# Opening stage of a two-layer hybrid trunk: remainders on VectorE, squares summed on TensorE, rotary angles first, loads in another order

## The chip, the cores and the metric

The kernel runs on one core of one Trainium2 chip. The metric is the device time of one execution in microseconds (us); lower is better. One core has TensorE (PE; its weight loads are listed apart as PEld), VectorE (DVE), ScalarE (ACT), GpSimd (POOL) and SyncE (SP), which here only issues the loads and stores.

## What is computed

Two layers; each is a mixer (latent attention and a state-space part side by side) and a SwiGLU, both behind an RMSNorm that is shifted and scaled by a modulation vector. Only the start of layer 0 bears on the change:

```python
ang = positions.astype(f32)[..., None] * inv_freq          # rotary angles
cos, sin = jnp.cos(ang), jnp.sin(ang)
c_act = jax.nn.silu(c)                                     # (1, 1024)
for l in range(2):
    mod = c_act @ w_ada[l] + b_ada[l]                      # w_ada: 1024 x 6144
    sh1, sc1, g1, sh2, sc2, g2 = jnp.split(mod, 6, axis=-1)
    h = rmsnorm(x, norm1_w[l]) * (1.0 + sc1) + sh1         # x: 512 x 1024
    x = x + g1 * hybrid_mixer(h, cos, sin, w_in[l], ...)   # begins with h @ w_in, 1024 x 1960
    h = rmsnorm(x, norm2_w[l]) * (1.0 + sc2) + sh2
    x = x + g2 * swiglu(h, w_gate_up[l], w_down[l])
```

## The kernel before

Activations lie transposed, xT[channel in a block of 128, block k = 0..7, row 0..511]. Every large product is taken in three matmuls: an f32 operand is split into a rounded part ("hi", hh, hik) and the remainder (lo, hl, lok), and hi·hi, hi·lo and lo·hi are added up in PSUM. ScalarE makes the rounded parts; the remainders are subtractions on VectorE or GpSimd.

The opening stage of layer 0 first loads c (cb, on all partitions) and x in two halves of 256 rows, squares x on ScalarE (sq), adds the squares on VectorE, sums over channels by a matmul with ones (st for the first half, nst for the second) and turns the sums into row scales (na, then rs). Matmuls of ones with ones (`warm`) fill TensorE in between. It then takes eight steps, k = 0..7, one for each block of channels:

- load two 512 KB tiles of w_ada (raws, blocks 8 + k and k) and a 404 KB slab of w_in (rawk);
- each raws is multiplied by cb and summed on VectorE into one column of mods; the bias is added, and gn = (1 + scale) · norm weight;
- ht = xT · gn · rs on VectorE; hh and hu, the rounded and the full hidden, on ScalarE; hl = hu − hh on GpSimd (step 0 does each of these per half of the rows);
- hik, the rounded slab, on ScalarE, and lok = rawk − hik on GpSimd;
- 21 matmuls into seven PSUM banks st: four chunks of 128 rows against the first 424 columns of the slab, and three column tiles of 128 against all 512 rows.

In step 2, `small_tables` makes the rotary angles (24 short operations on pf, ang, kk, kh, kl on VectorE, then three sines on ScalarE) and the mask mkb. After step 7 the mixer goes on with the tiles lo_7 and lo_8 (remainders of the next two weight tiles, on GpSimd), copies rw out of the banks, convolutions (xbc) and further products wps. SyncE issues all loads in the order of the program; a load waits there until its buffer is free (six buffers for raws, three for rawk and the later raw, three each for hi and lo).

Outside the parts that are pinned to program order, a scheduler orders the instructions of each engine when the kernel is built. At run time each engine takes its own in that order and waits by semaphores.

Of the kernel before, what the change touches and what calls it, by code (L numbers as in the profile page):

```python
# [71 lines left out]
    'KHV': 0,  # L72
# [3 lines left out]
P = 128  # L76
S = 512
# [68 lines left out]
class Kept:  # L146
    """an engine; while kept, its instructions stay in the order they are written in"""
# [19 lines left out]
class Stream:  # L167
    """steps for the tensor engine; a step yields the time from which on the next should find its data"""
# [9 lines left out]
def drive(te, streams, back):  # L178
    """the steps of all streams: next comes the first stream in the list whose step should find its data,
    and a step of back where there is none"""  # L180
    te.pinned = True
    while streams:
        for s in streams + [back]:
            if s.ready is not None and s.ready() <= te.now:
                s.step()
                break
        else:
            te.now = min(s.ready() for s in streams + [back] if s.ready is not None)
            assert te.now < INF
        streams = [s for s in streams if s.ready is not None]  # L190
    te.pinned = False
# [3 lines left out]
def trunk(ctx, tc, xin, cin, pos, eye, consts, small, wada, ws, out):  # L195
# [39 lines left out]
    tc.keep_in_program_order(nc.scalar.preload_act_table_set("silu_and_others"))  # L235
    nc.sync.dma_start(cb, cin.partition_broadcast(P))
    xload(HALVES[0])
    xload(HALVES[1])
    nc.sync.dma_start(sm[0], small[0])
# [12 lines left out]
    def small_tables():  # L252
        ve.tensor_copy(idb, ident)
        mk = kc[:, K_MASK:K_MASK + P]
        for i in range(4):
            tc.keep_in_program_order(ge.tensor_copy(mkb[:, i, :], mk))
# [3 lines left out]
        ang, kk, kh, kl = (tiny(nm, n, 1) for nm in ("ang", "kk", "kh", "kl"))  # L260
# [19 lines left out]
        ve.tensor_scalar(ang, ang, pi, -pi, op0=ALU.min, op1=ALU.max)  # L280
        v4 = lambda t: t.rearrange("p (c f) -> p c f", f=16)
# [3 lines left out]
        ve.tensor_copy(cs2[:, :, 1, :], cs2[:, :, 0, :])  # L285

# [82 lines left out]
    def rsqrt(y, x, scale, name, a=None, out=None):  # L369
        """y = (x * scale + EPS) ** -0.5: exp(-ln / 2) and a Newton step"""  # L370
        if a is None:
            a = tiny(f"na_{name}", x.free_size())
        se.activation(y, x, AF.Ln, scale=scale, bias=eps)
        se.activation(y, y, AF.Exp, scale=-0.5)
        if isinstance(scale, float):
            ve.scalar_tensor_tensor(a, x, EPS / scale, y, op0=ALU.add, op1=ALU.mult)
            ve.scalar_tensor_tensor(a, a, -0.5 * scale, y, op0=ALU.mult, op1=ALU.mult)
        else:
            ve.tensor_scalar(a, x, scale, EPS, op0=ALU.mult, op1=ALU.add)
            ve.scalar_tensor_tensor(a, a, -0.5, y, op0=ALU.mult, op1=ALU.mult)  # L380
            ve.tensor_tensor(a, a, y, op=ALU.mult)
        ve.scalar_tensor_tensor(y if out is None else out, a, 1.5, y, op0=ALU.add, op1=ALU.mult)

    class Norm:
        """adaLN over the columns of xT: squares added up tile by tile, then the row scale and the hidden"""
# [16 lines left out]
        def scale(self, sl, ps=None, rb=None):  # L402
            """(mean square + eps) ** -0.5 of the rows in sl, on all partitions"""
# [55 lines left out]
    def mixer(l, h, rows, first):  # L459
        s_ = sm[l]  # L460
        with tc.tile_pool(name=f"mx{l}", bufs=1) as mp:
# [14 lines left out]
            def decays():  # L476
                """time steps and decays, [step in chunk, (chunk, head)]"""
# [40 lines left out]
            def dense():  # L518
                """the rest of W_in, then the first half of the rows of W_out, tile by tile"""
# [56 lines left out]
            with tc.tile_pool(name=f"up{l}", bufs=2) as up, psum(f"u{l}", mm=2, ms=2, at=4):  # L576
# [3 lines left out]
                # latents, a chunk's rows on the partitions (their row scale follows after the up-projections)  # L580
# [33 lines left out]
                # rotary factors with the norm weights in them  # L614
# [7 lines left out]
                def rope(x, cw, sw, shape, name, re=ve):  # L622
                    """in place on x[..., 32]"""
# [109 lines left out]
            with tc.tile_pool(name=f"s2{l}", bufs=2) as sp, psum(f"v{l}", ms=2, sc=2, pt=1, op=1, mm=2):  # L733
# [12 lines left out]
                # attention over (chunk, heads), in three steps  # L746
# [34 lines left out]
                def values(c, h0, g):  # L781
                    """two heads at a time, one in each half of the columns of the array: channels on the partitions"""
# [39 lines left out]
                def norms():  # L822
                    """one over the sums of the probabilities, turned to where the channels are; then the products' split"""
# [19 lines left out]
                # the state space part, chunk by chunk  # L843
# [148 lines left out]
    def out_proj(l, mix, nrm, sl, kept):  # L992
        """one half of the rows; the weight tiles that lie on chip at its end are kept for the other half"""
# [93 lines left out]
    for l in range(L):  # L1087
        if l == 0:
            with tc.tile_pool(name="s0", bufs=6) as s0, psum("s", ms=1, st=NCH + NC0):
# [23 lines left out]

                def load(k):
# [178 lines left out]
```

## Time and profile before

| quantity | value |
|---|---|
| three timed runs | 1287.88 us median (1286.55 to 1293.02) |
| profiled execution | span 1284.9 us (the page gives its span alone) |
| PE busy | 1211.4 us, 94% of the span |
| DVE, ACT, POOL busy | 49%, 40%, 41% |
| chain that ended last | PE 38%, DVE 4%, ACT 2%, POOL 1%, DMA 1% |
| DMA | 162.34 MB, mean 126 GB/s |

The span is the time from the first to the last instruction of one profiled execution; the timed runs take some us more, since they hold what lies around it. Busy shares are means over all stages. The opening stage, up to the last matmul of step 7, takes the first 77.6 us.

### The profile page before, as it was taken

How to read it: one execution, taken by the hardware profiler on the slowest of the kernel's cores; microseconds unless marked ns; L12 is line 12 of the kernel's file. 1: busy time of each engine (PE TensorE's matmuls, PEld its weight loads, DVE VectorE, ACT ScalarE, POOL GpSimd, SP SyncE). 2: the span in 40 equal slices, each digit the busy share in tenths (PEclk: the TensorE clock that was granted, in tenths of full speed). 3: DMA queues.
4: the chain of work that ended last, by engine and by line, in shares of the span. 5: the costliest groups of instructions: out<-in, count | busy, mean ns of one | idle time of the engine just before them, and what ended most of it. 6: DMA issues, size and time to landing. Idle time of an engine off the chain costs nothing. (4 is left out here: it accounts for less than half of the span.)

```text
span 1284.9 us, 16463 instructions
## 1 busy us (share of the span) xinstructions
PE 1211.4 (94%) x6343; PEld 1005.1 (78%) x6344; DVE 634.1 (49%) x1128; ACT 519.9 (40%) x896; POOL 531.1 (41%) x310
## 2 busy tenths in 40 slices
PE   6889796889999999999998999979999999999998
PEld 6768674689888888888887887659988888888888
DVE  6979778879245545211128885576821111110100
ACT  4366774435322222222226668654532222222110
POOL 2651145263676666523333232346333333333231
PEclk9899898899999999999999899999999999999999
DMA  9433352464477777423223222103333332323331
GB/s 321 154 125 102 114 164 99 150 200 143 129 241 238 239 240 237 134 87 97 96 71 107 83 79 70 34 33 91 124 115 99 90 106 84 102 94 107 115 101 40
DMA packets 47855, 162.34 MB, mean 126 GB/s; under 512 B 5344, under 2 KB 8224, under 8 KB 47776
## 3 DMA queue, kind: packets, MB, share of 16 engines
q1 hardware_dynamic: 47776, 161.29, 38.8%
q8 instruction: 50, 0.82, 0.3%
q14 instruction: 29, 0.24, 0.1%
HBM read 159.14 MB, written 2.13 MB: 126 GB/s over the span
## 5 line engine op out<-in xcount | busy, mean ns | idle before, releaser
L292 POOL TENSOR_TENSOR lo<-raw,hi 128x1024 fp32r<-128x1024 f32 x108 | 272.6, 2524 | 338.6 <-ACT hi L156 338.5
L156 ACT CAST hi<-raw 128x1024 fp32r<-128x1024 f32 x179 | 188.0, 1051 | 500.8 <-issue 183.5
L140 PE MATMUL gup<-hl,hi 128*128 128x512 f32 (+1 forms) x736 | 280.4, 381 | 0.0
L140 PE MATMUL gup<-hh,lo 128*128 128x512 f32 (+1 forms) x736 | 279.9, 381 | 0.0
L140 PE MATMUL gup<-hh,hi 128*128 128x512 f32 (+1 forms) x736 | 278.6, 381 | 0.0
L156 DVE TENSOR_TENSOR lo<-raw,hi 128x1024 fp32r<-128x1024 f32 x71 | 88.9, 1253 | 152.6 <-ACT hi L156 150.8
L140 PEld LDWEIGHTS gup<-hh,lo 128*128 128x128 f32 x736 | 139.1, 189 | 26.5
L140 PEld LDWEIGHTS gup<-hl,hi 128*128 128x128 f32 x736 | 139.0, 189 | 26.0 <-DVE hl L156 0.2
L140 PEld LDWEIGHTS gup<-hh,hi 128*128 128x128 f32 x736 | 138.4, 189 | 26.2
L156 DVE SCALAR_TENSOR_TENSOR rawa<-rawa,cb 128x1024 f32<-128x1024 f32 x77 | 111.0, 1443 | 76.7 <-DMA rawa<-wada 76.5
L140 PE MATMUL dps<-ah,hi 128*128 128x512 f32 x308 | 121.8, 396 | 0.0
L140 PE MATMUL dps<-al,hi 128*128 128x512 f32 x308 | 121.8, 396 | 0.0
L140 PE MATMUL dps<-ah,lo 128*128 128x512 f32 x308 | 121.8, 396 | 0.0
L156 DVE TENSOR_TENSOR sg<-sg,gup 128x512 f32<-128x512 f32 x44 | 30.3, 688 | 179.6 <-PE gup L140 173.5
L440 POOL TENSOR_TENSOR al<-sg,ah 128x512 fp32r<-128x512 f32 x44 | 67.6, 1535 | 97.2 <-ACT ah L156 93.6
L140 PE MATMUL ops<-hh,hi 128*128 128x256 f32 x256 | 74.4, 290 | 3.1 <-ACT hi L156 1.5
L140 PE MATMUL ops<-hl,hi 128*128 128x256 f32 x256 | 72.5, 283 | 1.0 <-POOL hl L440 1.0
L140 PE MATMUL wps<-hh,hi 128*128 128x512 f32 x168 | 70.8, 422 | 2.4 <-DVE xbc L156 2.4
L140 PE MATMUL ops<-hh,lo 128*128 128x256 f32 x256 | 72.5, 283 | 0.3 <-POOL lo L292 0.3
L140 PEld LDWEIGHTS dps<-al,hi 128*128 128x128 f32 x308 | 57.9, 188 | 14.1
L140 PEld LDWEIGHTS dps<-ah,hi 128*128 128x128 f32 x308 | 57.9, 188 | 14.0
L140 PEld LDWEIGHTS dps<-ah,lo 128*128 128x128 f32 x308 | 57.9, 188 | 13.9
(303 smaller groups left out, 2103.3 us busy)
## 6 DMA issues: line engine op xcount, KB each, us to landing
raw<-ws SPq DMA_DIRECT2D x181, 512.0 KB, 3.5
rawa<-wada SPq DMA_DIRECT2D x80, 512.0 KB, 4.4
raws<-wada SPq DMA_DIRECT2D x16, 512.0 KB, 5.3
ar<-ard SPq DMA_DIRECT2D x8, 512.0 KB, 3.9
rawk<-ws SPq DMA_DIRECT2D x8, 404.0 KB, 5.4
xT<-xin SPq DMA_DIRECT2D x8, 256.0 KB, 5.9
out<-xT SPq DMA_DIRECT2D x7, 256.0 KB, 2.6
rawr<-ws SPq DMA_DIRECT2D x4, 424.0 KB, 3.2
```

Of the source, the lines that this page charges most:

```text
L140: self._put(self.tc.nc.tensor.matmul(out, lhsT, rhs, **kw), 4 * n if rhs.dtype == F32 else n)
L156: i = f(*args, **kw)
L292: (eng or ve).tensor_tensor(lo[:, :n], raw[:, :n], hi[:, :n].bitcast(F32), op=ALU.subtract)
L440: (eng or ve).tensor_tensor(lo, src, hi.bitcast(F32), op=ALU.subtract)
```

## The change

Only the opening stage's code is edited. The remainders hl and lok are made on VectorE; hl is taken from ht, its shift and hh in one instruction, so that hu is not made. The squares are no longer added on VectorE: TensorE sums eight blocks for each half, and VectorE makes half of the second half's squares. The angles are computed at the start, the sines before the table for logarithm and exponential is loaded, and gn takes one instruction with a prepared gb. Positions and frequencies are loaded first, then the first half of x, cb, the small weights and the second half of x. The third `warm` is gone.

```diff
+    nc.sync.dma_start(posi, pos)
+    nc.sync.dma_start(kc[:, K_FREQ:NK], consts[:, K_FREQ:NK])
+    xload(HALVES[0])
     nc.sync.dma_start(cb, cin.partition_broadcast(P))
-    xload(HALVES[0])
+    nc.sync.dma_start(sm[0], small[0])
     xload(HALVES[1])
-    nc.sync.dma_start(sm[0], small[0])
...
-                def stat(sl):
+                def squares(sl):
                     sq = s0.tile([P, KT, S // 2], F32, name=f"sq01{sl.start}", tag="sq", bufs=2)
                     for k in range(0, KT, 2):
-                        se.activation(sq[:, k:k + 2], xT[:, k:k + 2, sl], AF.Square)
-                        if k > 0:
-                            ve.tensor_tensor(sq[:, 0:2], sq[:, 0:2], sq[:, k:k + 2], op=ALU.add)
-                    for j in range(2):
-                        te.matmul((nst if sl.start else sps[-2])[:, 0:S // 2], ones, sq[:, j], start=j == 0, stop=j == 1)
+                        x = xT[:, k:k + 2, sl]
+                        if sl.start and k > 2:
+                            ve.tensor_tensor(sq[:, k:k + 2], x, x, op=ALU.mult)
+                        else:
+                            se.activation(sq[:, k:k + 2], x, AF.Square)
+                    return sq
+
+                def stat(sl, sq):
+                    for k in range(KT):
+                        te.matmul((nst if sl.start else sps[-2])[:, 0:S // 2], ones, sq[:, k], start=k == 0, stop=k == KT - 1)
...
                         ada1(0, t, s0.tile([P, 8, P], F32, name=f"raws{t}", tag="raws"))
-                        ada_fin(0, t, t + 1)
-                    return slab(wraw(f"k{k}"), wk0[k], f"k{k}", NS0, ge)
+                        m = mods[0][:, t:t + 1]
+                        if t < 8:
+                            ve.tensor_tensor(m, m, sm[0][:, C_BADA + t:C_BADA + t + 1], op=ALU.add)
+                        else:
+                            ve.scalar_tensor_tensor(gn[0][:, k:k + 1], m, nw1[:, k:k + 1], gb[:, k:k + 1], op0=ALU.mult, op1=ALU.add)
+                    return slab(wraw(f"k{k}"), wk0[k], f"k{k}", NS0)
...
+                angles()
                 warm(PLAN['WU'])
+                sq = squares(HALVES[0])
                 se.activation(cb, cb, AF.Silu)
-                stat(HALVES[0])
+                stat(HALVES[0], sq)
+                sq = squares(HALVES[1])
+                sines()
                 exp_ln_tables()
+                ve.scalar_tensor_tensor(gb, sm[0][:, C_BADA + 8:C_BADA + 16], 1.0, nw1, op0=ALU.add, op1=ALU.mult)
+                stat(HALVES[1], sq)
+                scale(HALVES[0])
+                scale(HALVES[1])
                 warm(PLAN['WV'])
-                scale(HALVES[0])
-                stat(HALVES[1])
-                scale(HALVES[1])
-                warm(PLAN['WW'])
...
                     for sl in HALVES if k == 0 else (FULL,):
-                        last = hid(0, 1, h, k, rs0[:, sl], sl, ge)
-                    for sl in HALVES if k < PLAN['KHV'] else (FULL,):
+                        last = hid(0, 1, h, k, rs0[:, sl], sl)
                         mms(k, w, sl)
                     if k == PLAN['STK']:
                         with tc.issue_after(last.ins):
-                            small_tables()
-                        exp_ln_tables()
+                            ve.tensor_copy(idb, ident)
+                            se.copy(cs2[:, :, 1, :], cs2[:, :, 0, :])
```

How the instructions stand then, at three places. VectorE, one step of the loop (raws13 and raws5 are the two w_ada tiles of step 5, ht015 its scaled x); before:

```order
L156 SCALAR_TENSOR_TENSOR raws13_459,mods0_92<-raws13_459,cb_69 128x1024
L156 TENSOR_TENSOR mods0_92<-mods0_92,sm0_72 128x1
L156 SCALAR_TENSOR_TENSOR gn0_94<-mods0_92,sm0_72 128x1
L156 SCALAR_TENSOR_TENSOR ht015_0_474<-xT_71,gn0_94,rs0_116 128x512
L156 SCALAR_TENSOR_TENSOR raws5_464,mods0_92<-raws5_464,cb_69 128x1024
L156 TENSOR_TENSOR mods0_92<-mods0_92,sm0_72 128x1
```

The same stretch of the change, from the tile raws13 on:

```order
L155 SCALAR_TENSOR_TENSOR raws13_441,mods0_96<-raws13_441,cb_69 128x1024
L155 SCALAR_TENSOR_TENSOR hl_101<-ht014_0_416,mods0_96,hh_100 128x512
L155 SCALAR_TENSOR_TENSOR gn0_98<-mods0_96,sm0_72,gb_121 128x1
L155 SCALAR_TENSOR_TENSOR raws5_445,mods0_96<-raws5_445,cb_69 128x1024
L155 TENSOR_TENSOR lok5_451<-rawk5_449,hik5_450 128x808
L155 TENSOR_TENSOR mods0_96<-mods0_96,sm0_72 128x1
L155 SCALAR_TENSOR_TENSOR ht015_0_455<-xT_71,gn0_98,rs0_120 128x512
```

The step gains two instructions on VectorE, hl (of the step before, behind the next step's first tile) and lok (behind its second); GpSimd's stream has none of either left: its first large instruction is lo_7, behind the four small products that put the norm weights into the sines and cosines and the mask's four casts.

VectorE, from the row scales to the first hidden (na and rs are the scale's working tiles, 0 and 256 the two halves); before:

```order
L156 TENSOR_TENSOR mods0_92<-mods0_92,sm0_72 128x1
L156 SCALAR_TENSOR_TENSOR ht010_0_216<-xT_71,gn0_94,rs0_116 128x256
L156 CAST pf_341<-posi_70 128x4
L156 TENSOR_TENSOR ang_343<-pf_341,kc_67 128x64
L156 SCALAR_TENSOR_TENSOR na01_256_177<-nst0_114,na01_256_177 128x256
L156 TENSOR_SCALAR kk_344<-ang_343 128x64
L156 SCALAR_TENSOR_TENSOR na01_256_177<-na01_256_177 128x256
L156 TENSOR_SCALAR kk_344<-kk_344 128x64
L156 SCALAR_TENSOR_TENSOR rs0_116<-na01_256_177 128x256
L156 TENSOR_SCALAR kh_345<-kk_344 128x64
L156 SCALAR_TENSOR_TENSOR ht010_256_222<-xT_71,gn0_94,rs0_116 128x256
```

The same place in the change:

```order
L155 SCALAR_TENSOR_TENSOR na01_0_199<-st5_116,na01_0_199 128x256
L155 SCALAR_TENSOR_TENSOR raws8_225,mods0_96<-raws8_225,cb_69 128x1024
L155 SCALAR_TENSOR_TENSOR na01_0_199<-na01_0_199 128x256
L155 SCALAR_TENSOR_TENSOR gn0_98<-mods0_96,sm0_72,gb_121 128x1
L155 SCALAR_TENSOR_TENSOR rs0_120<-na01_0_199 128x256
L155 SCALAR_TENSOR_TENSOR na01_256_205<-nst0_118,na01_256_205 128x256
L155 SCALAR_TENSOR_TENSOR raws0_229,mods0_96<-raws0_229,cb_69 128x1024
L155 SCALAR_TENSOR_TENSOR na01_256_205<-na01_256_205 128x256
L155 TENSOR_TENSOR mods0_96<-mods0_96,sm0_72 128x1
L155 TENSOR_TENSOR lok0_235<-rawk0_233,hik0_234 128x808
L155 SCALAR_TENSOR_TENSOR rs0_120<-na01_256_205 128x256
L155 SCALAR_TENSOR_TENSOR ht010_0_239<-xT_71,gn0_98,rs0_120 128x256
```

The angle operations between the scale's steps are gone from here, to the head of VectorE's stream, and lok of step 0 stands ahead of the last step of the second half's scale.

ScalarE, from its first table load; before:

```order
L235 ACT_TABLE_LOAD
L156 ACTIVATE cb_69<-cb_69 128x1024
L156 ACTIVATE sq010_136<-xT_71 128x512 x4
L250 ACT_TABLE_LOAD
L156 ACTIVATE na01_0_161<-st5_112,eps_86 128x256
L156 ACTIVATE na01_0_161<-na01_0_161 128x256
L156 ACTIVATE sq01256_167<-xT_71 128x512 x4
```

The same of the change:

```order
L234 ACT_TABLE_LOAD
L155 ACTIVATE sq010_167<-xT_71 128x512 x4
L155 ACTIVATE cb_69<-cb_69 128x1024
L155 ACTIVATE sq01256_181<-xT_71 128x512 x2
L155 ACTIVATE sn2_93<-kh_95 128x4x16 x2
L155 ACTIVATE cs2_92<-ang_94 128x4x16
L251 ACT_TABLE_LOAD
L155 ACTIVATE na01_0_199<-st5_116,eps_88 128x256
L155 COPY cs2_92<-cs2_92 128x4x16
L155 ACTIVATE na01_0_199<-na01_0_199 128x256
L155 ACTIVATE na01_256_205<-nst0_118,eps_88 128x256
L155 ACTIVATE na01_256_205<-na01_256_205 128x256
```

The squares of the first half go ahead of silu(cb), three sines stand ahead of the second table load, and the scales of both halves follow it.

From step 7's last matmul on, the orders of both kernels agree, apart from a few instructions that stand one to three places earlier or later among VectorE's and ScalarE's next thirty (one 768-wide remainder, ul, comes ahead of the third copy rw).

## Rows read from the trace of the kernel before

**Rows 1.** Windows: busy us (instructions) of PE, PEld, DVE, ACT, POOL; clock; DMA share; GB/s.

```profile
0.00:7.00 7.00, 5.64 (x36) 5.45 (x36) 0.17 (x2) 2.89 (x4) 0.20 (x4) 1.00 0.71 200
7.00:12.00 5.00, 2.02 (x9) 1.85 (x10) 2.08 (x3) 3.74 (x6) 0.00 (x0) 0.87 1.09 371
12.00:22.00 10.00, 9.00 (x66) 8.64 (x65) 9.47 (x21) 5.04 (x10) 2.73 (x2) 0.89 1.03 404
...
49.00:55.00 6.00, 5.74 (x15) 5.03 (x16) 5.82 (x8) 2.09 (x3) 4.54 (x4) 0.50 0.56 175
55.00:66.00 11.00, 9.82 (x45) 7.96 (x43) 10.56 (x16) 3.83 (x6) 5.53 (x4) 0.99 0.30 101
```

**Rows 2.** Timeline of VectorE, one step: start, us, operation, tiles, shape, count.

```profile
57.80 1.22 DVE L156 SCALAR_TENSOR_TENSOR raws<-raws,cb 128x1024 f32<-128x1024 f32 x1
...
59.53 1.63 DVE L156 SCALAR_TENSOR_TENSOR ht<-xT,gn,rs 128x512 f32<-128x512 f32 x1
61.08 2.94 DVE L156 SCALAR_TENSOR_TENSOR raws<-raws,cb 128x1024 f32<-128x1024 f32 x1
...
64.07 0.16 DVE L156 TENSOR_TENSOR mods<-mods,sm 128x1 f32<-128x1 f32 x1
64.15 1.22 DVE L156 SCALAR_TENSOR_TENSOR raws<-raws,cb 128x1024 f32<-128x1024 f32 x1
```

**Rows 3.** Timeline of GpSimd: step 0, a middle step, the last and what follows.

```profile
24.15 0.73 POOL L433 TENSOR_TENSOR hl<-hu,hh 128x256 fp32r<-128x256 f32 x1 [2.01 <-ACT hu L156]
...
59.33 1.28 POOL L433 TENSOR_TENSOR hl<-hu,hh 128x512 fp32r<-128x512 f32 x1 [2.74 <-ACT hu L156]
60.57 2.38 POOL L300 TENSOR_TENSOR lok<-rawk,hik 128x808 fp32r<-128x808 f32 x1
...
72.02 1.26 POOL L433 TENSOR_TENSOR hl<-hu,hh 128x512 fp32r<-128x512 f32 x1 [2.73 <-ACT hu L156]
73.25 4.83 POOL L292 TENSOR_TENSOR lo<-raw,hi 128x1024 fp32r<-128x1024 f32 x2
```

**Rows 4.** Timeline of VectorE at five other places.

```profile
28.13 0.74 DVE L156 SCALAR_TENSOR_TENSOR ht<-xT,gn,rs 128x512 f32<-128x512 f32 x1
...
36.63 0.49 DVE L156 SCALAR_TENSOR_TENSOR ang<-kk,ang 128x64 f32<-128x64 f32 x2
...
76.58 1.52 DVE L156 COPY dtr<-rw 128x16 f32<-128x16 f32 x1 [0.24 <-ACT rw L156]
...
652.18 1.23 DVE L156 TENSOR_TENSOR lo<-raw,hi 128x1024 fp32r<-128x1024 f32 x1 [8.54 <-ACT hi L156]
...
681.35 0.48 DVE L156 SCALAR_TENSOR_TENSOR hl<-ht,mods,hh 128x256 fp32r<-128x256 f32 x1
```

**Rows 5.** Timeline of ScalarE from the first loads to the first slab.

```profile
5.33 1.06 ACT L156 ACTIVATE cb<-cb 128x1024 f32<-128x1024 f32 x1 [3.32 <-DMA cb<-cin]
6.30 2.76 ACT L156 ACTIVATE sq<-xT 128x512 f32<-128x512 f32 x4
9.07 1.28 ACT L250 ACT_TABLE_LOAD   x1
11.37 0.47 ACT L156 ACTIVATE na<-st,eps 128x256 f32<-128x256 f32 x1 [1.01 <-PE st L140]
...
15.47 0.86 ACT L156 CAST hik<-rawk 128x808 fp32r<-128x808 f32 x1 [1.09 <-DMA rawk<-ws]
```

**Rows 6.** Timeline of TensorE: sum of squares, step 7, the products after it.

```profile
9.98 1.35 PE L140 MATMUL st<-sq,ones 128*128 128x256 f32 x4 [3.29 <-DVE sq L156]
...
73.34 0.46 PE L140 MATMUL st<-hik,hl 128*128 128x424 f32 x1 [1.50 <-POOL hl L433]
...
77.64 0.40 PE L140 MATMUL wps<-hh,hi 128*128 128x512 f32 x1
...
85.65 0.60 PE L140 MATMUL wps<-hh,hi 128*128 128x512 f32 x1 [2.37 <-DVE xbc L156]
```

**Rows 7.** The load of the positions (2 KB): us from issue to landing.

```profile
DMA to landing us min/median/max: 5.9/5.9/5.9
```

More of the change, by code (lines that the diff above doesn't have):

```diff
@@ L71 @@
     'WV': 14,
-    'KHV': 0,
     'STK': 2,
@@ L250, in exp_ln_tables, with angles @@
         tc.keep_in_program_order(nc.scalar.preload_act_table_set("natural_log_exp_and_others"))
[L252 to L256, printed above, removed]
+    ang, kh = (cp.tile([P, NCH * 16], F32, name=n) for n in ("ang", "kh"))
+    def angles():
         n = NCH * 16
@@ L259, in small_tables @@
         ve.tensor_copy(pf, posi)
-        ang, kk, kh, kl = (tiny(nm, n, 1) for nm in ("ang", "kk", "kh", "kl"))
+        kk, kl = (tiny(nm, n, 1) for nm in ("kk", "kl"))
         ve.tensor_tensor(ang.rearrange("p (c f) -> p c f", f=16), pf.unsqueeze(2).broadcast_to([P, NCH, 16]),
@@ L280, in small_tables, with sines @@
         ve.tensor_scalar(ang, ang, pi, -pi, op0=ALU.min, op1=ALU.max)
+    def sines():
         v4 = lambda t: t.rearrange("p (c f) -> p c f", f=16)
@@ L284, in small_tables @@
         se.activation(cs2[:, :, 0, :], v4(ang), AF.Sin)
-        ve.tensor_copy(cs2[:, :, 1, :], cs2[:, :, 0, :])
     def wsplit(raw, name, n, eng=None):
@@ L1100, in trunk @@
                 wk0 = ws[0, 0:7].rearrange("b p m -> (b p m)").rearrange("(k p m) -> k p m", p=P, m=7 * P)
-                def stat(sl):
+                def squares(sl):
                     sq = s0.tile([P, KT, S // 2], F32, name=f"sq01{sl.start}", tag="sq", bufs=2)
                     for k in range(0, KT, 2):
-                        se.activation(sq[:, k:k + 2], xT[:, k:k + 2, sl], AF.Square)
-                        if k > 0:
-                            ve.tensor_tensor(sq[:, 0:2], sq[:, 0:2], sq[:, k:k + 2], op=ALU.add)
-                    for j in range(2):
-                        te.matmul((nst if sl.start else sps[-2])[:, 0:S // 2], ones, sq[:, j], start=j == 0, stop=j == 1)
+                        x = xT[:, k:k + 2, sl]
[7 more added lines that the diff above has]
+                        te.matmul((nst if sl.start else sps[-2])[:, 0:S // 2], ones, sq[:, k], start=k == 0, stop=k == KT - 1)
                 def scale(sl):
                     nrm.scale(sl, nst if sl.start else sps[-2], rs0[:, sl])
+                nw1 = sm[0][:, C_N1:C_N1 + 8]
+                gb = s0.tile([P, 8], F32, name="gb", bufs=1)
                 def load(k):
@@ L1130, in trunk @@
                 te.pinned = True
+                angles()
                 warm(PLAN['WU'])
+                sq = squares(HALVES[0])
                 se.activation(cb, cb, AF.Silu)
-                stat(HALVES[0])
+                stat(HALVES[0], sq)
+                sq = squares(HALVES[1])
+                sines()
                 exp_ln_tables()
+                ve.scalar_tensor_tensor(gb, sm[0][:, C_BADA + 8:C_BADA + 16], 1.0, nw1, op0=ALU.add, op1=ALU.mult)
+                stat(HALVES[1], sq)
+                scale(HALVES[0])
+                scale(HALVES[1])
                 warm(PLAN['WV'])
-                scale(HALVES[0])
-                stat(HALVES[1])
-                scale(HALVES[1])
-                warm(PLAN['WW'])
-                te.pinned = False
-                ve.kept = se.kept = False
+                te.pinned = ve.kept = se.kept = False
                 for k in range(KT):
                     if k == 1:
+                        nc.sync.dma_start(kc[:, 0:K_FREQ], consts[:, 0:K_FREQ])
                         nc.sync.dma_start(ki, eye)
-                        nc.sync.dma_start(posi, pos)
-                        nc.sync.dma_start(kc, consts)
                     w = load(k)
                     for sl in HALVES if k == 0 else (FULL,):
-                        last = hid(0, 1, h, k, rs0[:, sl], sl, ge)
-                    for sl in HALVES if k < PLAN['KHV'] else (FULL,):
+                        last = hid(0, 1, h, k, rs0[:, sl], sl)
                         mms(k, w, sl)
@@ L1153, in trunk @@
                         with tc.issue_after(last.ins):
-                            small_tables()
-                        exp_ln_tables()
+                            ve.tensor_copy(idb, ident)
+                            se.copy(cs2[:, :, 1, :], cs2[:, :, 0, :])
+                            for i in range(4):
+                                tc.keep_in_program_order(ge.tensor_copy(mkb[:, i, :], kc[:, K_MASK:K_MASK + P]))
                 ada_q.extend([(0, t) for t in list(range(16, 24)) + list(range(32, 40)) + list(range(24, 32)) + list(range(40, 48))])
```

## The prediction

> **What bounds the kernel now.** I read the windows first. TensorE is busy 94% of the span, but the opening stage is another matter: from 55 to 66 us VectorE is busy 10.56 of 11 us while DMA moves 101 GB/s, against 404 GB/s from 12 to 22 us [rows 1]. So once the first loads are in, the steps are not held by loads. The timeline of VectorE then shows a step that repeats: the second raws of a step starts at 57.80, and the next at 64.15, 6.35 us later [rows 2]. The same instruction on a 512 KB tile takes 1.22 us at 57.80 and 2.94 us at 61.08, and ht takes 1.63 us at 59.53 [rows 2] where it took 0.74 at 28.13 [rows 4]. The timeline of GpSimd says what is beside the long ones: hl from 59.33 to 60.61 beside ht, and lok from 60.57 to 62.95 beside raws [rows 3]. VectorE is busy all the time and yet about 2.6 us of a step (2.94 − 1.22, and 1.63 − 0.74) are stretch. TensorE waits for the end of this chain: in step 7 it waits for hl, which ends at 73.28 [rows 3], starts its first hl product at 73.34 and has the stage done at 77.64 [rows 6]. What counts is when the last hl is ready; I compare it before and after in three pieces.
>
> **Front, up to hl of step 0.** Before, the second half's hl ends at 24.88 (24.15 + 0.73) [rows 3]. After, the loads up to the second half of x are 2.76 MB (x 2.10, cb 0.52, small 0.13, and 10 KB for positions and frequencies). At 200 GB/s up to 7 us and 371 GB/s from there [rows 1] 1.40 MB are in at 7.0 us, x's first half with cb (1.58 MB) at 7.5, and all 2.76 MB at 10.7. ScalarE squares the first half while cb comes in, then takes silu(cb) (1.06 [rows 5]) from 7.5 to 8.6, two squares of the second half at 0.69 each (2.76 for four [rows 5]), held by their landing, to 10.0, three sines of 64 columns (under the 0.47 of a 256-column operation [rows 5]; I take 0.25 each) to 10.8, the table load (1.28 [rows 5]) to 12.1, then Ln and Exp of the first half (0.47 each at most) to about 13.1 with the short copy of the cosines between them.
>
> Three things must be ready by then. The angles: 24 operations at 0.25 (two in 0.49 [rows 4]) are 6.0 us; they can start when the positions are in. No row shows that load on an idle queue; under load it took 5.9 us [rows 7]. It now goes first at 0.74 us or so. I take 3 us, so the angles end near 10, which is when the last blocks of x land for VectorE's two squares (0.69 each, to 11.4). The sums: 16 matmuls instead of 4. Two of them, four instructions, took 1.35 us with the filling of the pipeline in it [rows 6]; I take 0.4 for one, so eight are 3.2 us on a TensorE that had only `warm` to do, and the second half's last ones wait for the squares and end near 12.2. And raws: it was used at about 15 us, and rawk's hik began at 15.47, waiting for its load [rows 5]; the loads ahead of both are the same bytes plus 10 KB.
>
> From 13.1 VectorE goes through the listed order: six scale steps of 0.34 (0.42, less 0.08 of overlap), three raws at 1.22, lok, two one-column operations, and two ht and two hl of half width (0.48 [rows 4], 0.40 apart). Next operations start 0.08 before the last ends (64.07 + 0.16 against 64.15 [rows 2]). For lok on VectorE no row has the width 808: 1024 columns take 1.23 and 512 take 0.74 [rows 4], so 808 take 1.02, or 0.94 apart. The sum is 2.0 + 3.7 + 0.9 + 0.2 + 1.6 = 8.4, plus small waits: hl ends near 21.7. **Gain 3.2 us.**
>
> **Seven steps.** Before, from 24.88 to 73.28: 48.4 us, 6.9 each, since steps 1 to 4 also carry the angles and the mask. After, a step on VectorE is raws 1.22, hl 0.66, gn 0.1, raws 1.22, lok 0.94, mods 0.1, ht 0.66: 4.9 us, with GpSimd idle. hl's input hh is made by ScalarE (about 0.7, as a square of 512 columns) while VectorE has the next raws, so it costs nothing; if that cover went, 0.8 a step. The last step has no next raws: gn to ht 3.1, hh 0.8 in the open, hl 0.74: 4.7. So 6 × 4.9 + 4.7 = 34.1. One stretch stays: lo_7 on GpSimd needs buffers that step 5's matmuls free, at about 50, and so falls on step 7's raws, lok or ht. The lok that ran 2.38 us stretched raws by 1.72 [rows 2, 3]; I add 1.7. lo_8 comes behind hh of step 7 and should miss hl. 35.8 in all. **Gain 12.6 us.**
>
> On that stretch the Trainium skill (SBUF — State Buffer, Who interferes with whom) says that a VectorE instruction with two SBUF inputs and a GpSimd instruction that reads SBUF exclude each other for the whole instruction. The row shows 1.72 us lost beside 2.38; by the rule it could be all of 2.38, and the gain 0.7 less. The measured 1.72 stands in my sum.
>
> **End.** In step 7 the order has four hi products ahead of the wait instead of one, so 17 of the 20 matmuls that took 4.30 us (73.34 to 77.64 [rows 6]) come behind hl: 3.65. **Gain 0.65 us.** Behind the stage the streams are nearly as before: eight blocks of wps, then TensorE waits 2.37 us for the convolutions [rows 6]. VectorE's part ahead of them loses a stalled copy (dtr, 1.52 for 16 columns [rows 4]) and gets a 768-wide remainder of about 1.0: I take 0, with −1.5 to +1.5 as bounds.
>
> At nothing I put the table loads, hu's ScalarE time, the squares' adds and gb: ScalarE has 3.83 us to do in 11 [rows 1] and stays far from full. The steps' loads are 1.46 MB each, 3.6 us at 404 GB/s, hidden under 4.9; without that cover a step would be as long as its loads.
>
> Sum: 3.2 + 12.6 + 0.65 = 16.4. The profiled span of 1284.9 becomes 1268.5; the runs' median is 3.0 above that span, and I carry that: **1271.5 us**, 1.3% less.
>
> **Bounds.** Positions: between 0 and 5.9 us to land; the late end puts the angles' end at 12.6, the sines at 12.9 and the scales about 2 us later; the early end gains nothing, since x lands then. A sum's matmul: at the row's 0.68 all sixteen would take 10.9 us and end near 17.6, which puts VectorE's scale steps of the second half about 2.5 later. lok: between 0.66 (512 columns) and 1.15 (1024), 7 steps: +2.0 to −1.5, and I sit on the width. lo_7: 0 to 2.4. TensorE's clock: idle stretches before a step have ended in half clock (0.50 from 49 to 55 us [rows 1], behind waits for hl); between the last `warm` (ends near 15.5) and step 0 (near 20) TensorE idles again. Step 0 at half clock costs up to 3 us on TensorE, which 0.4 us a step (4.9 − 4.5) takes back, mostly hidden: 0 to 2. Together with the ±1.5 behind the stage the gain runs from about 10 to about 20.5: 1267.5 to 1278.
>
> **Rivals.**
> (a) *Loads take over.* If the steps' loads came at 250 GB/s instead of 404, a step would be 5.85, seven of them 6.7 longer: gain 9.7, time 1278. For it: windows below 200 GB/s [rows 1]; against: in those VectorE was never idle (5.82 of 6 us), so nothing was asked for faster.
> (b) *The stretch isn't GpSimd's.* Then the instructions keep their lengths and hl and lok come on top: 6.35 + 0.66 + 0.94 = 7.95 a step, hl ends at 21.7 + 55.7 = 77.4, the stage at 81.0: 3.4 us later, 1291, no change that counts. For it: nothing but that long ones also had loads beside them; against: 1.22 at 57.80, with GpSimd idle.
> (c) *Slower: TensorE stays at half clock.* A step is 21 matmuls, 4.5 us at full clock (20 in 4.30), 9.0 at half. If the gap ahead of step 0 drops the clock and short waits keep it there, eight steps from 20 end at 92, 14 us later: 1302. It decides from an average step of 7.2 us on ((77.6 − 20) / 8). For it: 0.50 from 49 to 55; against: 0.99 from 55 to 66, with a wait in each step.
> (d) *Swallowed later*, by a load or a due time behind the stage that doesn't move: half the gain, 1280. Against: what follows waits for banks, weights' buffers and VectorE, which all move along.
>
> **Chances.** A difference under 0.5% (6.4 us) is about what can't be told from none. Forecast, 1267.5 to 1276: 0.72. (a) or a late front, 1276 to 1281: 0.14. (d) at its worst and (b), 1281 to 1294: 0.10. (c): 0.04. So faster 0.87, same 0.09, slower 0.04. For eight in ten the range is 1267 to 1278.
>
> **What would show it.** Right: hl of step 7 ends at 56 to 59 us, the first wps at 60 to 63; raws stays at 1.22 in every step but the one beside lo_7; successive second raws stand 4.8 to 5.1 apart; GpSimd has nothing large before 50 us. Wrong: raws over 2 us with GpSimd idle (b), clock at 0.5 over several steps (c), VectorE idle before raws for DMA (a), the first hl later than 24 us (front), or the first wps 15 us earlier and the end of the kernel not (d).

## The result and the profile after

The change takes 1272.76 us (median of four runs, 1271.95 to 1275.59) against 1288.12 us (four runs beside them, 1286.55 to 1293.02): 0.9879 of the time, 95% interval 0.9858 to 0.9900. The forecast of 1271.5 us and its range held. The profiled execution took 1273.26 us with a span of 1271.5 us, against the 1284.9 of before. So the spans differ by 13.4 us and the medians by 15.4: executions of one kernel scatter by several us, the longer ones at a lower mean clock of TensorE (the change's four: spans of 1270.1 us at 0.982 to 1273.8 at 0.976), and the stage marks inside a trace are the sharper measure.

The windows of the change, in the stretches of [rows 1] (busy us and instructions of PE, PEld, DVE, ACT, POOL; clock; DMA share; GB/s):

```profile
0.00:7.00 7.00, 5.95 (x37) 5.95 (x38) 3.60 (x19) 3.17 (x4) 0.20 (x4) 1.00 0.57 158
7.00:12.00 5.00, 3.51 (x17) 2.74 (x15) 1.47 (x8) 1.65 (x2) 0.00 (x0) 1.00 0.97 292
12.00:22.00 10.00, 6.84 (x44) 6.24 (x44) 7.04 (x15) 5.70 (x13) 4.62 (x8) 1.00 1.04 403
49.00:55.00 6.00, 5.94 (x29) 5.05 (x28) 6.00 (x13) 2.43 (x3) 0.62 (x1) 1.00 0.42 131
55.00:66.00 11.00, 8.74 (x35) 7.35 (x34) 8.24 (x15) 5.77 (x18) 4.55 (x2) 0.84 0.41 122
```

Two things differ at once. The first loads came slower than before, 158 and 292 GB/s where it was 200 and 371. And from 55 to 66 us TensorE's clock is down to 0.84 of full speed, with VectorE busy 8.24 of 11 us.

The timeline of VectorE (start, us, operation, tiles, shape, count, idle time before it and what ended it):

```profile
14.13 1.51 DVE L155 TENSOR_TENSOR sq<-xT 128x512 f32<-128x512 f32 x2 [5.45 <-DMA xT<-xin]
...
24.27 0.87 DVE L155 SCALAR_TENSOR_TENSOR hl<-ht,mods,hh 128x256 fp32r<-128x256 f32 x2
...
48.97 1.22 DVE L155 SCALAR_TENSOR_TENSOR raws<-raws,cb 128x1024 f32<-128x1024 f32 x1
...
50.11 0.99 DVE L155 TENSOR_TENSOR lok<-rawk,hik 128x808 fp32r<-128x808 f32 x1
...
51.09 0.74 DVE L155 SCALAR_TENSOR_TENSOR ht<-xT,gn,rs 128x512 f32<-128x512 f32 x1
51.76 1.21 DVE L155 SCALAR_TENSOR_TENSOR raws<-raws,cb 128x1024 f32<-128x1024 f32 x1
...
52.90 0.74 DVE L155 SCALAR_TENSOR_TENSOR hl<-ht,mods,hh 128x512 fp32r<-128x512 f32 x1
...
53.70 1.22 DVE L155 SCALAR_TENSOR_TENSOR raws<-raws,cb 128x1024 f32<-128x1024 f32 x1
...
54.84 3.19 DVE L155 TENSOR_TENSOR lok<-rawk,hik 128x808 fp32r<-128x808 f32 x1
...
59.55 0.75 DVE L155 SCALAR_TENSOR_TENSOR hl<-ht,mods,hh 128x512 fp32r<-128x512 f32 x1 [0.79 <-ACT hh L155]
...
71.14 1.40 DVE L155 SCALAR_TENSOR_TENSOR xbc<-st,sm,xbc 128x509 f32<-128x509 f32 x2
```

A step now reads as foretold: raws 1.22, lok 0.99, ht 0.74 and hl 0.74, with no instruction longer than it is alone ("stretched" below), and the second raws of two steps (48.97 and 53.70) are 4.73 us apart, where [rows 2] had 6.35. Two rows break the pattern. VectorE idles 5.45 us for x's second half, up to 14.13, and lok of step 7 takes 3.19 us. GpSimd's timeline says what is beside that lok (lo_7, then lo_8):

```profile
54.38 2.80 POOL L293 TENSOR_TENSOR lo<-raw,hi 128x1024 fp32r<-128x1024 f32 x1 [33.22 <-ACT hi L155]
60.53 2.37 POOL L293 TENSOR_TENSOR lo<-raw,hi 128x1024 fp32r<-128x1024 f32 x1 [3.35 <-ACT hi L155]
```

ScalarE and the loads of the front, to be read beside [rows 5] and [rows 7] (the second fence: size of one load, median us from issue to landing):

```profile
10.98 1.06 ACT L155 ACTIVATE cb<-cb 128x1024 f32<-128x1024 f32 x1 [2.52 <-DMA cb<-cin]
12.63 1.38 ACT L155 ACTIVATE sq<-xT 128x512 f32<-128x512 f32 x2 [0.59 <-DMA xT<-xin]
...
14.46 1.28 ACT L251 ACT_TABLE_LOAD   x1
15.76 0.47 ACT L155 ACTIVATE na<-st,eps 128x256 f32<-128x256 f32 x1
```

```profile
cb<-cin SPq DMA_DIRECT2D x1, 512.0 KB, 7.3
...
posi<-pos SPq DMA_DIRECT2D x1, 2.0 KB, 1.6
```

The positions landed in 1.6 us, not 3. But cb, which stands behind x's first half, took 7.3 us and was ready at 10.98, not at 7.5; x's second half came at 12.63 and later; the table load started at 14.46 and so ended at 15.74, where the prediction had 12.1. TensorE's end of the stage, to be read beside [rows 6]:

```profile
54.94 0.35 PE L139 MATMUL st<-lok,hh 128*128 128x424 f32 x1
...
59.57 1.78 PE L139 MATMUL st<-hik,hh 128*128 128x424 f32 x4 [2.26 <-ACT hh L155]
61.15 0.56 PE L139 MATMUL st<-hik,hl 128*128 128x424 f32 x1
...
65.50 0.40 PE L139 MATMUL wps<-hh,hi 128*128 128x512 f32 x1
...
72.68 0.47 PE L139 MATMUL wps<-hh,hi 128*128 128x512 f32 x1 [1.55 <-DVE xbc L155]
...
79.68 0.74 PE L139 MATMUL kvps<-hi,lh 128*128 128x512 f32 x2 [0.63 <-ACT lh L155]
```

In step 7 TensorE now waits 2.26 us (for hh, which stands behind the long lok), and its next products of 424 columns take 0.56 us where they took 0.35 in step 6: half clock. The first wps starts at 65.50 and the second tile of them at 72.68, after 1.55 us of waiting; before, it was 77.64 and 85.65, after 2.37.

### The profile page after: what moved, and what is told of

Same layout as the page of the kernel before. It is cut to its first block, busy times and chain, and to the rows that moved or that the text cites. A ratio compares the mean times of both kernels' runs of the same rounds, so it can differ in the third digit from the quotient of the medians.

```text
span 1271.5 us, 16417 instructions
## 1 busy us (share of the span) xinstructions
PE 1205.4 (95%) x6340; PEld 1002.3 (79%) x6341; DVE 623.0 (49%) x1133; ACT 511.4 (40%) x884; POOL 502.3 (40%) x293
## 5 line engine op out<-in xcount | busy, mean ns | idle before, releaser
L139 PEld LDWEIGHTS gup<-hl,hi 128*128 128x128 f32 x736 | 138.3, 188 | 26.4 <-DVE hl L155 0.4
L441 POOL TENSOR_TENSOR al<-sg,ah 128x512 fp32r<-128x512 f32 x44 | 71.5, 1626 | 96.9 <-ACT ah L155 96.9
```

The costliest lines, as they stand in the source:

```text
L139: self._put(self.tc.nc.tensor.matmul(out, lhsT, rhs, **kw), 4 * n if rhs.dtype == F32 else n)
L441: (eng or ve).tensor_tensor(lo, src, hi.bitcast(F32), op=ALU.subtract)
```

## The experiments

Twelve kernels ran, in three sets; the kernel before ran beside each set (medians 1285.53, 1285.63 and 1287.39 us). Times are medians; the ratio is to the kernel before of the same set, with its 95% interval. The marks are from each kernel's one profile, in us: the end of hl of step 0 (second half) and of step 7, the start of the first wps, of the second tile of wps, and of the first latent product kvps behind it.

| kernel | hl, step 0 | hl, step 7 | wps | 2nd tile | kvps | median | ratio |
|---|---|---|---|---|---|---|---|
| before | 24.88 | 73.28 | 77.64 | 85.65 | 94.25 | | |
| the change | 25.14 | 60.30 | 65.50 | 72.68 | 79.68 | 1272.76 | 0.9879 |
| rem_back_gpsimd | 25.56 | 69.88 | 73.23 | 82.40 | 91.92 | 1284.75 | 0.9995 (0.9977 to 1.0014) |
| only_rem_vector | 26.4 | 62.52 | 66.87 | 74.95 | 83.56 | 1275.21 | 0.9914 (0.9886 to 0.9942) |
| lok_gpsimd | 26.95 | 63.87 | 67.67 | 76.55 | 86.36 | 1280.09 | 0.9942 (0.9924 to 0.9960) |
| hl_gpsimd | 26.12 | 60.60 | 64.41 | 73.10 | 81.42 | 1276.90 | 0.9918 (0.9887 to 0.9950) |
| load_cb_first | 21.90 | 57.07 | 62.42 | 69.15 | 76.15 | 1268.47 | 0.9870 (0.9842 to 0.9898) |
| load_x_first | 24.08 | 57.97 | 63.31 | 70.04 | 77.01 | 1270.49 | 0.9881 (0.9846 to 0.9915) |
| load_cb_last | 24.48 | 58.37 | 62.16 | 70.19 | 78.77 | 1271.04 | 0.9884 (0.9862 to 0.9906) |
| lo7_vector | 24.71 | 57.68 | 61.50 | 72.20 | 81.78 | 1274.86 | 0.9914 (0.9888 to 0.9939) |
| change_again | 24.20 | 59.36 | 64.69 | 71.47 | 78.48 | 1274.02 | 0.9894 (0.9869 to 0.9918) |
| lo7_behind_hh | 24.71 | 57.67 | 61.49 | 71.19 | 80.42 | 1269.22 | 0.9868 (0.9844 to 0.9892) |
| cb_first_lo7_behind | 22.96 | 55.93 | 59.71 | 69.44 | 79.15 | 1273.18 | 0.9884 (0.9854 to 0.9913) |
| warm_longer | 24.01 | 59.17 | 62.99 | 70.98 | 77.99 | 1274.87 | 0.9894 (0.9867 to 0.9921) |

change_again is the change unaltered. Its six runs reach from 1269.97 to 1278.95 us, so differences of 2 or 3 us in the median can't be told there, and the marks are used for them. From kvps to the end of the span the fourteen profiled executions take 1188.1 to 1194.4 us, so that an earlier kvps shows in the time only where it is several us. The marks scatter too: kernels with the same front end hl of step 0 at 24.01 to 25.14, and a later mark is best read as its distance from that one.

> The changed kernel once more, unaltered, beside the other runs of this set, so that they can be set against it under the same conditions: ratio 0.987 to 0.990 to the kernel before, hl of step 0 at 25.1, last hl at 60.3, first product with the next weights at 65.5.

### What the step is made of

My theory: before, VectorE's long instructions are long because GpSimd works beside them, and the remainders' move alone makes the gain. The rival (b): they are long for another reason. Four kernels go between before and after in both directions.

**rem_back_gpsimd**: the change with both remainders, and hu, as before.

```diff
-                    return slab(wraw(f"k{k}"), wk0[k], f"k{k}", NS0)
+                    return slab(wraw(f"k{k}"), wk0[k], f"k{k}", NS0, ge)
...
-                        last = hid(0, 1, h, k, rs0[:, sl], sl)
+                        last = hid(0, 1, h, k, rs0[:, sl], sl, ge)
```

> The change with both remainders (hl and lok) made on GpSimd again, and hu with them; front, angles and loads stay as changed. Theory (the steps' gain is the stretch that GpSimd's subtractions put on VectorE): a step is 6.3 to 6.4 us again instead of 4.73, raws and ht are long beside hl and lok, the last hl comes 10 to 12 us later than in the change, and the time is 1281 to 1285 us. Rival (the gain is the angles' leaving the steps, or the front): steps stay at about 4.7 to 5 and the time within 2 us of the change's 1272.8.

The last steps are back at 6.34 to 6.37 us (GpSimd's hl starts at 55.89, 62.26 and 68.60). VectorE's timeline of this kernel, a raws alone and the raws beside lok, then GpSimd's lok:

```profile
23.07 1.21 DVE L155 SCALAR_TENSOR_TENSOR raws<-raws,cb 128x1024 f32<-128x1024 f32 x1
...
26.03 2.93 DVE L155 SCALAR_TENSOR_TENSOR raws<-raws,cb 128x1024 f32<-128x1024 f32 x1
```

```profile
25.52 2.35 POOL L301 TENSOR_TENSOR lok<-rawk,hik 128x808 fp32r<-128x808 f32 x1
```

The stage ends 4.4 us before that of the kernel before, but kvps only 2.3 us, and the time is the same within 0.2%. The last hl came 9.6 us later than in the change, a little less than expected. So the other edits together (angles, squares, loads) give nothing that the whole time shows.

**only_rem_vector**: the kernel before with the remainders alone on VectorE (the same two lines the other way round).

> The kernel before with nothing but the two remainders moved to VectorE; angles stay in the steps, and front and loads are as before. Theory: steps without angles are 4.7 to 4.9 us; the 24 angle operations cost VectorE another 6 us in the middle steps; step 0's hl ends near 24.9 as before, the last hl near 66 instead of 73.3, the time 1279 to 1283 us. Rival (remainders on VectorE only add 1.6 us a step): 1288 to 1300 us.

It did better than I expected: the last hl at 62.52, not near 66, and 0.9914 of the time. Of the 12.1 us by which the change's stage ends earlier, 10.8 are here already (77.64 to 66.87).

**lok_gpsimd** and **hl_gpsimd**: the change with one of the two remainders back on GpSimd (one of the two lines above each).

> The change with lok alone back on GpSimd. Theory: VectorE loses 0.91 us of its own a step and gets a stretch by lok on GpSimd. If the stretch is the 1.7 us seen in the kernel before, a step is 5.5 us and the last hl 6 us later than in the change; if lok excludes VectorE for its whole 2.4 us, 6.2 us and 10 us later. Time 1278 to 1283 us. Rival (VectorE is simply full): steps shorten to 3.9 us and the time falls below 1270.

> The change with hl alone (and hu) back on GpSimd. Theory: VectorE loses 0.66 us a step and gets a stretch of 0.9 (as ht had beside hl before) to 1.3: a step of 4.9 to 5.4 us, the last hl 1 to 5 us later, the time 1274 to 1278 us. Rival (VectorE is simply full): steps of 4.1 us and the time below 1270.

The steps took 5.50 and 5.09 us, as expected. The last hl came only 3.6 and 0.3 us later than in the change, less than expected, since lo_7 comes behind the last hl in both and stretches nothing in step 7. In lok_gpsimd the stretch falls on gn, which has one column and took 0.21 us in the change. The timelines of VectorE and of GpSimd in a middle step of lok_gpsimd:

```profile
47.57 1.89 DVE L155 SCALAR_TENSOR_TENSOR gn<-mods,sm,gb 128x1 f32<-128x1 f32 x1
```

```profile
47.44 2.01 POOL L301 TENSOR_TENSOR lok<-rawk,hik 128x808 fp32r<-128x808 f32 x1 [3.49 <-ACT hik L155]
```

A one-column instruction waits out nearly the whole subtraction. That is a cost for each meeting of two instructions, and not a share of VectorE's own length; rival (b) falls with it. The trace of the kernel before had the same at step 0, where a one-column add of mods takes 1.85 us beside GpSimd's lok, and 0.16 us in a later step [rows 2]:

```profile
16.73 1.85 DVE L156 TENSOR_TENSOR mods<-mods,sm 128x1 f32<-128x1 f32 x1
```

```profile
16.41 2.15 POOL L300 TENSOR_TENSOR lok<-rawk,hik 128x808 fp32r<-128x808 f32 x1 [15.97 <-ACT hik L156]
```

hl_gpsimd has one thing better than the change: no lok is stretched, and the first wps starts at 64.41, 1.1 us before the change's. It loses that again behind the stage (second tile at 73.10): the 16-column copy dtr, 0.17 us in the change, takes 2.33 us at 63.02, while GpSimd makes lo_7 and lo_8 (60.55 to 65.31).

### The front

Front theories: L1, the two loads of short rows at the head cost about a microsecond of all that follows; L2, cb's load is slow where x stands ahead of it, and holds up ScalarE and the loads behind it. The edits move lines of the list of loads (load_cb_last also puts silu(cb) behind the sines).

```diff
+    nc.sync.dma_start(cb, cin.partition_broadcast(P))
     nc.sync.dma_start(posi, pos)
     nc.sync.dma_start(kc[:, K_FREQ:NK], consts[:, K_FREQ:NK])
     xload(HALVES[0])
-    nc.sync.dma_start(cb, cin.partition_broadcast(P))
```

> The changed kernel with the load of the silu input cb put ahead of all others (then positions and frequencies, x's first half, the small rows, x's second half). In the changed kernel cb landed at 11.0 us, x's second half at 12.6 to 14.1, and step 0's hl ended at 25.1. Theory L2 (the broadcast load of cb, queued among x's loads, is what is slow and holds back what stands behind it): cb lands at about 5, x's second half at 11 to 12, hl of step 0 ends at about 22.5, and the end of the opening stage comes 2 to 2.5 us earlier, 1270 to 1271 us in all. Theory L1 (the loads of short rows at the head of the queue cost over a microsecond of every later load): hl of step 0 stays at about 25 and the time at 1272 to 1273.

> The changed kernel with x's first half put ahead of the positions and frequencies; cb stays behind those. L1 (the short rows at the head cost time): the first half's squares end over 1 us earlier than the changed kernel's 8.5, hl of step 0 ends at about 24, positions land at about 4 and the angles still end before the squares' sums are wanted. L2 (cb is slow behind x): cb still lands at about 10 to 11 and hl of step 0 stays at about 25. Time 1271.5 to 1273 either way.

> The changed kernel with cb loaded behind both halves of x (its silu moved behind the squares and sines on ScalarE). L2: x's second half lands at 10 to 11 us, its squares end before 12, hl of step 0 ends at 22 to 23 unless cb, which lands at 12 to 13, holds up ScalarE's logarithm; time 1270 to 1271. L1: x's second half still lands at 12.5 to 14 and hl of step 0 ends at 25 or later; time 1272 to 1274.

With cb first, ScalarE's timeline and the load's landing:

```profile
8.14 0.63 ACT L155 ACTIVATE sq<-xT 128x512 f32<-128x512 f32 x1 [0.53 <-DMA xT<-xin]
8.68 1.04 ACT L155 ACTIVATE cb<-cb 128x1024 f32<-128x1024 f32 x1
9.62 1.13 ACT L155 ACTIVATE sq<-xT 128x512 f32<-128x512 f32 x2
...
11.21 1.28 ACT L251 ACT_TABLE_LOAD   x1
```

```profile
cb<-cin SPq DMA_DIRECT2D x1, 512.0 KB, 3.6
```

cb lands in 3.6 us instead of 7.3, silu ends at 9.72 instead of 12.04, and hl of step 0 ends at 21.90 (22.96 in cb_first_lo7_behind, with the same loads). The unaltered front gave 24.01 to 25.14 in its five executions (the change, change_again, lo7_vector, lo7_behind_hh, warm_longer). So cb first gains 1.0 to 3.2 us, as L2 has it. But it takes the short rows from the head too, and L1 can't be set aside. With x first, where cb still stands behind x's first half, that half's squares are done at 7.36 instead of 8.47, and cb is ready by 9.11 (10.01 to 10.98 in the five). Its hl of step 0 ends at 24.08, but that mark can't be compared: in load_x_first and load_cb_last the scheduler put a second raws of step 1 ahead of it. At hl of step 1 the work ahead is the same in all of them. The change, then load_x_first:

```profile
29.13 0.74 DVE L155 SCALAR_TENSOR_TENSOR hl<-ht,mods,hh 128x512 fp32r<-128x512 f32 x1
```

```profile
26.79 0.74 DVE L155 SCALAR_TENSOR_TENSOR hl<-ht,mods,hh 128x512 fp32r<-128x512 f32 x1
```

It ends at 27.53 with x first, at 26.63 and 27.69 with cb first, at 27.94 with cb last, and at 28.74 to 29.87 in the five. So moving the short rows alone (x first) gains 1.2 to 2.3 us there, cb last 0.8 to 1.9 and cb first 1.0 to 3.2: both theories hold in part, and their shares can't be told in a scatter of 1.1 us. With cb last x's second half is squared by 12.0, but cb lands only when silu starts, at 12.63, and holds the logarithm in its turn. Why cb's load, which reads one 4 KB row for all 128 partitions, is slower behind x, none of these runs tells.

### The end of the stage

If lo_7 beside lok costs 2.2 us and TensorE its clock, then moving lo_7 should give both back. **lo7_vector** makes it on VectorE behind step 7's hl; **lo7_behind_hh** leaves it on GpSimd but rounds hi_7 behind step 7's hh; **cb_first_lo7_behind** is that with cb loaded first.

In lo7_vector (last is step 7's hl; the pin orders the subtraction behind it on VectorE):

```diff
-                ... mtile(0, B_IN + 4 + t, h, f"wps0{t}", eng=ge)
+                ... mtile(0, B_IN + 4 + t, h, f"wps0{t}", eng=ge if t > NC0 else None, pin=last if t == NC0 else None)
```

In lo7_behind_hh (hhi[0] is step 7's hh; the pin orders the cast behind it on ScalarE):

```diff
-        se.copy(hi[:, :n], raw[:, :n])
+        with tc.issue_after(pin.ins) if pin else nullcontext():
+            se.copy(hi[:, :n], raw[:, :n])
...
-                ... mtile(0, B_IN + 4 + t, h, f"wps0{t}", eng=ge)
+                ... mtile(0, B_IN + 4 + t, h, f"wps0{t}", eng=ge, pin=hhi[0] if t == NC0 else None)
```

> The changed kernel with the remainder of the first weight tile behind step 7 (lo_7, on GpSimd and 2.8 us beside step 7's one-column work) on VectorE, behind step 7's hl. Theory of the changed kernel's end: the stretch of lok goes (2.2 us), the last hl ends near 58.1 instead of 60.3, TensorE no longer idles 2.3 us in step 7 and so keeps its full clock there, and the first product with the next weights starts near 62 instead of 65.5; with the 3.5 us carried to the end the time is 1269 to 1270. Rival: on VectorE the subtraction comes in the way of what follows the stage there, the start of those products stays at 64 to 65.5, and the time stays at 1272 to 1273.

> The changed kernel with the high part hi_7 of the first weight tile behind step 7 rounded on ScalarE behind step 7's hh instead of before it, so that its remainder lo_7, still on GpSimd, runs behind step 7's one-column work and VectorE gets no work more. If the GpSimd subtraction beside lok is what costs the stage's end its 2.2 us and TensorE its clock: lok of step 7 0.99, last hl at about 58.1, first product with the next weights at about 61.8, the second tile of them (72.7 in the changed kernel) at 69 to 70, time 1269 to 1270. Rival: VectorE's convolution, which frees the second tile's bank, isn't earlier for it (as where lo_7 went to VectorE), the second tile starts at 71.5 or later, and the time stays within 1 us of the changed kernel's.

> Both edits that moved the stage's marks: cb loaded first and hi_7 behind step 7's hh. If the two add up: hl of step 0 at 21.9, last hl at about 54.9, first product with the next weights at 58.5 to 59, the second tile at 66 to 67, and 1265 to 1267 us. If VectorE's convolution takes back the second edit's gain: the second tile at 68.5 to 69.5 and 1267.5 to 1269, as with cb first alone.

The first half of the theory is shown: in all three the lok of step 7 takes 0.99 us, and step 7 runs at full clock. The last hl of lo7_vector and lo7_behind_hh ends at 57.68 and 57.67, and the first wps starts at 61.50 and 61.49, 4.0 us before the change's (3.6 us, counted from hl of step 0). The second half is not: the second tile waits for the bank that VectorE's convolution frees, and that moved by 0.5 and 1.5 us. TensorE's timeline of lo7_behind_hh, then VectorE's and GpSimd's:

```profile
61.49 0.39 PE L139 MATMUL wps<-hh,hi 128*128 128x512 f32 x1
...
71.19 0.77 PE L139 MATMUL wps<-hh,hi 128*128 128x512 f32 x1 [4.10 <-DVE xbc L155]
71.76 0.63 PE L139 MATMUL wps<-hl,hi 128*128 128x512 f32 x1
...
80.42 0.74 PE L139 MATMUL kvps<-hi,lh 128*128 128x512 f32 x2 [0.63 <-ACT lh L155]
```

```profile
54.41 0.99 DVE L155 TENSOR_TENSOR lok<-rawk,hik 128x808 fp32r<-128x808 f32 x1
...
60.40 3.16 DVE L155 SCALAR_TENSOR_TENSOR ul<-raw,sm,uh 128x768 fp32r<-128x768 f32 x1
...
69.64 1.40 DVE L155 SCALAR_TENSOR_TENSOR xbc<-st,sm,xbc 128x509 f32<-128x509 f32 x2
```

```profile
57.90 4.84 POOL L294 TENSOR_TENSOR lo<-raw,hi 128x1024 fp32r<-128x1024 f32 x2 [37.17 <-ACT hi L155]
```

The stretch only moved on. lo_7 and lo_8 now run back to back, and ul takes 3.16 us beside them. In the change it comes when lo_8 has ended, at 62.90:

```profile
63.32 1.01 DVE L155 SCALAR_TENSOR_TENSOR ul<-raw,sm,uh 128x768 fp32r<-128x768 f32 x1
```

The convolution that frees the bank starts 8.15 us behind the first wps (61.49 to 69.64), where the change has 5.64; the 2.15 us of ul are most of that. TensorE waits 4.10 us and then multiplies at half clock (0.63 us for 512 columns, against 0.39), so that kvps starts at 80.42, 0.7 us after the change's. In lo7_vector the subtraction itself (1.22 us) and two instructions that the scheduler now puts ahead of the last convolution take the gain: second tile 72.20 after a wait of 5.08, kvps 81.78. Its rival was right that nothing comes of it, but looked for the loss ahead of the first wps. cb_first_lo7_behind has its second tile at 69.44, no earlier than cb first alone (69.15), as its second case said; its median, 1273.18, is above both of its cases, with an interval that overlaps that of cb first. The median of lo7_behind_hh, 1269.22, was the lower of the set, while its profiled execution was its slowest, 1276.36; its interval overlaps that of change_again, and its marks give no reason for a gain.

**warm_longer** (34 rounds of the filling products instead of 14) keeps TensorE at full clock in step 0.

```diff
-    'WV': 14,
+    'WV': 34,
```

> The changed kernel with 34 instead of 14 rounds of the products that keep TensorE busy ahead of step 0. If the half clock in step 0 (24.8 to 28.5) is hidden, since TensorE waits for hh again from step 4 on: step 0 at full clock or with a shorter half-clock stretch, last hl (60.3) and first product with the next weights (65.5) where they were, time 1271.5 to 1274. Rival: it wasn't hidden, and both come 1 to 2 us earlier.

TensorE's timeline around step 7 of that kernel:

```profile
58.44 1.03 PE L139 MATMUL st<-hik,hh 128*128 128x424 f32 x4 [2.27 <-ACT hh L155]
...
62.99 0.39 PE L139 MATMUL wps<-hh,hi 128*128 128x512 f32 x1
...
70.98 0.47 PE L139 MATMUL wps<-hh,hi 128*128 128x512 f32 x1 [2.38 <-DVE xbc L155]
```

From 24 to 29 us its clock was 1.00, against 0.66 in the change, and the steps kept their 4.73 us: the half clock of step 0 was hidden. Unexpectedly the same wait of 2.27 us in step 7 did not cost it the clock (four products in 1.03 us, against 1.78), and the first wps came 3.8 us behind the last hl instead of 5.2. load_cb_last, with the 14 rounds of the change and the same long lok, kept its full clock there too, after the same wait:

```profile
57.64 1.03 PE L139 MATMUL st<-hik,hh 128*128 128x424 f32 x4 [2.26 <-ACT hh L155]
```

So lo_7 beside lok makes the wait, and the wait alone does not settle the clock. In warm_longer the second tile then waits for the convolution, 2.38 us (ul met lo_8 there and took 1.69), and the time is that of the change: the rival's 1 to 2 us came at one mark and not at the end.

## Why the prediction held, step by step

- **Front, gain 3.2: mis-sized, measured −0.3** (24.88 to 25.14). The sum let the loads go at 200 and 371 GB/s in whatever order, and they went at 158 and 292; above all it took cb as bytes in a row (in at 7.5), where it was ready at 10.98. silu ended at 12.04, not at 8.6, and that is the whole 3.4 us of the miss. The chain from there (two squares, three sines, table load, logarithm, the list of VectorE) was right: 13.1 us to the end of hl, both foretold (8.6 to 21.7) and measured (12.04 to 25.14).
- **Seven steps, gain 12.6: right, measured 13.2.** 48.4 us became 35.2 (25.14 to 60.30), with 28.5 for the first six where I had 29.4. This step carries the result, and only_rem_vector shows that the move alone does it: 36.1 us (26.4 to 62.52), with the angles still in the steps.
- **lo_7's stretch, 1.7: measured 2.2** (lok 3.19 against 0.99), in lok and not in raws. GpSimd's subtraction took 2.80 us beside it, against 2.37 alone: it begins at 54.38 beside raws, which ends at 54.92, and lok, from 54.84, ends 0.85 us after it. The Trainium skill (SBUF — State Buffer, Who interferes with whom) says that a VectorE instruction with two SBUF inputs contends with a GpSimd instruction that reads SBUF, and calls the port pair that they share an exclusive lock. The traces agree: the 2.38 that the prediction drew from the rule was nearer to 2.20 than my 1.7, and the one column of gn in lok_gpsimd took 1.89 us beside 2.01.
- **End, gain 0.65: wrong, measured −0.84** (5.20 us from the last hl to the first wps, against 4.36). The first wps, foretold for 60 to 63, came at 65.50. The 17 matmuls behind hl were right, but their clock wasn't: I had seen a wait end in half clock ahead of a step [rows 1] and allowed for it in step 0 alone. The long lok made such a wait in step 7, and half clock followed (not so in load_cb_last and warm_longer). lo7_behind_hh, without the wait, took 3.82. The wait ahead of the 0.50 in [rows 1] was one for hh, and not for hl as the prediction reads it:

```profile
47.01 1.07 PE L140 MATMUL st<-hik,hh 128*128 128x424 f32 x4 [3.06 <-ACT hh L156]
```

- **Behind the stage, 0 (±1.5): measured +2.4 at kvps, +1.3 at the end.** The stage gains 12.1 us, kvps 14.6 (94.25 to 79.68), since the second tile's wait shrank from 2.37 to 1.55 and its half clock went (8.60 us from there to kvps became 7.00); the spans differ by 13.4. The 1.2 us between are within the scatter of what follows kvps.

The sum of 16.4 was thus 3.0 too large for the spans. The median came out nearer, 1.3 off, by luck: I added the 3.0 us that before's median lay above its profiled span, and the change's median lies 1.3 above its own. Of the signs, the hl of step 7 (60.30, foretold for 56 to 59), the first wps and the first hl (25.14, wrong later than 24) failed, as the terms above say; the steps (4.73, foretold 4.8 to 5.1) came out a little shorter.

Of the rivals, (a) fell: VectorE never waited for a load in a step after step 0. (b) fell with lok_gpsimd, and (c) because the half clock stayed in steps 0 and 7. (d) was not the change's way, but it was that of lo7_vector, lo7_behind_hh and warm_longer, which moved the first wps by 2.5 to 4.0 us and the end by nothing that can be told.

## What to carry to other kernels

Where VectorE and GpSimd work on SBUF side by side as here, count each meeting of two instructions as a wait of the later one for what is left of the earlier, and ask of every GpSimd instruction which VectorE instruction it will meet next; moving it away from one only helps if the next one has time to spare. When loads change places, a sum of bytes over a rate is not enough: the load of cb, which repeats one short row, took up to twice as long behind others (5.4 to 7.3 us) as ahead of them (3.6 to 4.6). And carry a gain on to the next wait for a buffer or bank, since a stage's end that comes 4 us earlier is worth nothing if that one stays.

## What was not expected of the hardware

- An instruction of one column (128x1) took 1.89 us beside a GpSimd subtraction of 2.01 us. The GpSimd instruction was longer too when it met a VectorE one: 2.80 us against 2.37.
- The 512 KB load of cb landed in 3.6 to 4.6 us ahead of all other loads, in 6.3 to 7.3 behind the short rows and x's first half, and in 5.4 in load_x_first, where the short rows stand behind that half too.
- A wait of TensorE of about 2.3 us was followed by half clock in step 7 of the change (2.26), in change_again, load_cb_first and load_x_first (2.26 each), and not in warm_longer (2.27) or load_cb_last (2.26). What differed between these stretches wasn't separated.
